# First-layer head outputs leave PSUM in one ScalarE copy: the square is taken from SBUF, and the sub-norm weight joins the product with the root

## The chip, the cores and the metric

The kernel runs on one core of one Trainium2 chip. The metric is device time in microseconds: 826.21 us is the median of three runs of the kernel before (824.39 to 827.17). A core has a matmul engine (TensorE; PE in the profile, PEld its weight loads), a vector engine (VectorE, DVE), an activation engine (ScalarE, ACT), a general engine (GpSimd, POOL) and a queue engine that issues DMAs (SyncE, SP). Each engine runs its own list of instructions in order and waits on semaphores for the others. Matmuls write to PSUM, which is cut into banks; everything else lives in SBUF.

## The reference

Two layers work on 512 latent tokens and 256 context tokens, 1024 wide. The change lies in the first layer, a differential attention with 8 heads, each with a 128-wide value and two 64-wide query/key pairs. Its core:

```python
o1 = sweep_attention(qq[..., 0, :], kk[..., 0, :], vv)
o2 = sweep_attention(qq[..., 1, :], kk[..., 1, :], vv)
o = o1 - lam * o2
o = rms_norm(o, subln_g) * (1.0 - lam_init)      # x * rsqrt(mean(x*x) + eps) * g, over a head's 128
o = o.reshape(o.shape[0], o.shape[1], BRANCH_WIDTH)
return (o * jax.nn.silu(gate)) @ w_out
```

Latent queries read all 768 keys, context queries only the 256 context keys. Around it stand the norms, adaptive shifts, scales and gates (`adaln`), and rotary positions. The second layer is a grouped-query attention with another code path, which the change does not touch.

## The kernel before, in words

**Precision.** Every matmul operand is split into a high and a low part (`h`, `whi`/`wlo`, `ah`/`al`, `vhi`/`vlo`), and three products are summed (`mm3`, L143 to L145; for the attention's second product `pv_mm`, L150). A split costs a cast on ScalarE and a subtraction on VectorE or GpSimd: weights at L213 (high) and L207 (low), values at L816 and after.

**PSUM.** There are four banks `bk` of 512 columns, handed out by least recent use: `trp()` takes one for a short time, `pj(n)` holds one as an accumulator until `close(o)` gives it back. Two double tiles `sc` hold attention scores. Whoever takes a bank waits until the last reader of its old contents is done.

**The first layer's attention.** For each head and each block of 128 queries, `unit` (L862 and after) makes both score sets (L880), takes their maximum (L885, VectorE), the exponential with its sum (L888, ScalarE), the reciprocal (L891), scales the first set (helper line L221, GpSimd), and combines `p = p0 + (-lambda/l1) p1` (L896, VectorE). The context queries have their own lines (L909 to L927). `tstep` transposes `p` (L945) and splits it: `ah` on ScalarE (L950), `al` on VectorE (L951). `mstep` multiplies with the values into a bank of 128 value rows by 256 queries. Each head has three such chunks of queries (two latent, one context): 24 outputs of 128x256 in all. After a head's last chunk, `subln` normalizes the 128x768 result: the column sum of squares by a matmul with ones (`colsum`, L378 to L382: cast on ScalarE, rest on GpSimd, two matmuls, result on all rows), logarithm (L979) and exponential (L981) on ScalarE give the root, VectorE multiplies (L982), and GpSimd multiplies with the gate `sz` (`gate_mul`, L839). The gate itself is made by `z_proj` (copy L850, and the steps L176 to L181 of a SiLU over ScalarE, VectorE and GpSimd). The last head has a form of its own, `subln_last` (L986 to L1000), in a piece of 512 and one of 256 columns, with the split for the out projection at once (L999, L1000); the other heads are split at L1026 and L1027.

**Order.** A planner in Python (`flow`) merges streams of steps (scores, transposes, second products, norms, and the adaptive rows at L736) by due times, and fills what is left with pieces of projections of later heads (queries and keys, values, gates). Then a scheduler at build time sets the order of each engine's list from priorities and its own estimate of durations. A changed instruction can therefore move others, on all engines.

**What the change touches.** `o` is the bank of a finished chunk, `gT[h]` the head's 128x768 result in SBUF, `ogs[h]` (`sq`) the tile of its squares, `subg` a column of 128 weights (the sub-norm's weight times 1 - lambda_init). At the end of a chunk ScalarE squares the bank (L968), VectorE multiplies it by `subg` (L969, through the helper `scaled`; `EG0 = 'v'` selects VectorE, and the profile shows it as L221 with `gT<-bk,subg`), and the bank is closed (L970).

Of the kernel before, what the change touches and what calls it, by code (L numbers as in the profile page):

```python
# [11 lines left out]
AF = mybir.ActivationFunctionType  # L12
ALU = mybir.AluOpType
# [54 lines left out]
EG0 = 'v'  # L68
# [8 lines left out]
def f32(ap):  # L77
    return ap.bitcast(F32)
# [3 lines left out]
def tile_backbone(  # L82
# [20 lines left out]
    nc = tc.nc  # L103
    uid = [0]

    def nm(s):
        uid[0] += 1
        return f"{s}_{uid[0]}"
# [15 lines left out]
    def trp():  # L124
        i = lru.pop(0)
        lru.append(i)
        return banks[i]

    def pj(n):
        i = lru.pop(0)  # L130
        o = banks[i][:, :n]
        held[id(o)] = (o, i)
        return o

    def close(o):
        lru.append(held.pop(id(o))[1])
# [10 lines left out]
    def pv_mm(o, vh, vl, c, ah, al, kt, first, last):  # L147
        terms = [(v, a, e) for v, a in ((vh, ah), (vl, ah), (vh, al)) for e in range(2)]
        for i, (v, a, e) in enumerate(terms):
            nc.tensor.matmul(o, v[:, kt + e, c], a[:, e * 256:e * 256 + 256], start=first and i == 0, stop=last and i == 5)  # L150
# [21 lines left out]
    subg = con.tile([P, 1], F32, name="subg")  # L172
# [44 lines left out]
    def scaled(eng, dst, src, s_):  # L217
        if eng == "a":
            nc.scalar.activation(dst, src, AF.Copy, scale=s_)
        else:  # L220
            (nc.vector if eng == "v" else nc.gpsimd).tensor_scalar(dst, src, s_, 1.0, ALU.mult, ALU.mult)  # L221
# [141 lines left out]
    def chunk(layer, tstep, mstep, kts, after, ts, ms):  # L363
        for i, kt in enumerate(kts):
            t = Step(lambda kt=kt: tstep(kt), 0.44, [(s_, LA[layer]) for s_ in after])
            if i:
                t.lag.append((ts[-1], LT[layer]))
            if len(ms) >= AB:
                t.lag.append((ms[-AB], 0.0))
            m = Step(lambda kt=kt: mstep(kt), 0.65, [(t, LM[layer])])  # L370
            ts.append(t)
            ms.append(m)
# [4 lines left out]
    def colsum(o, src, parts):  # L377
        hi, lo = parts  # L378
        nc.scalar.copy(hi, src)
        nc.gpsimd.tensor_tensor(lo, src, f32(hi), ALU.subtract)  # L380
        nc.tensor.matmul(o, ones_r, hi, start=True, stop=False)
        nc.tensor.matmul(o, ones_r, lo, start=False, stop=True)  # L382
# [53 lines left out]
    def htile():  # L436
        return hp.tile([P, T], F32R, tag="h", name=nm("h"), bufs=16)
# [277 lines left out]
    gT = [None] * KT  # L715

    with tc.tile_pool(name="t0", bufs=1) as t0:
# [118 lines left out]
        def gate_mul(h):  # L836
            done.add(h)
            if h in szt and (h, "o") in done:
                nc.gpsimd.tensor_tensor(gT[h], gT[h], szt[h], ALU.mult)  # L839
# [96 lines left out]
        def pv_steps(h, at, ch, after, ts, ms):  # L936
            kts = range(6) if ch < 2 else range(4, 6)
            st = {}

            def tstep(kt):  # L940
                tr = trp()
                for e in range(2):
                    j = kt + e - kts[0]
                    for i, a in enumerate(at):
                        nc.tensor.transpose(tr[:, e * 256 + i * P:e * 256 + (i + 1) * P], a[:, j * P:(j + 1) * P], ident)  # L945
                if h == 0 and ch == 0 and kt == 0:
                    t0.tile([P, 8], F32, name="pad_a")
                ah = t0.tile([P, 512], F32R, tag="ah", name=nm("ah"), bufs=AB)
                al = t0.tile([P, 512], F32R, tag="al", name=nm("al"), bufs=AB)
                nc.scalar.copy(ah, tr)  # L950
                nc.vector.tensor_tensor(al, tr, f32(ah), ALU.subtract)  # L951
                st[kt] = ah, al

            def mstep(kt):
                if kt == kts[0]:
                    st["o"] = pj(256)
                o = st["o"]
                ah, al = st[kt]
                vh, vl = vt[h]
                vc = slice((h % 2) * P, (h % 2) * P + P)  # L960
                pv_mm(o, vh, vl, vc, ah, al, kt, kt == kts[0], kt == kts[-2])
                if kt == kts[-2]:
                    if ch == 2:
                        pvdone.add(h)
                    sl = slice(ch * 256, ch * 256 + 256)
                    if ch == 0:
                        ogs[h] = t0.tile([P, T], F32, tag="sq", name=nm("sq"), bufs=1)
                    nc.scalar.activation(ogs[h][:, sl], o, AF.Square)  # L968
                    scaled(EG0, gT[h][:, sl], o, subg)  # L969
                    close(o)  # L970

            chunk(0, tstep, mstep, kts[::2], [after], ts, ms)

        def subln(h):
            sq, og = ogs[h], gT[h]
            for (a, b) in halves:
                o2 = pj(384)
                colsum(o2, sq[:, a:b], [t0.tile([P, 512], F32R, tag="tmp", name=nm("sqs"), bufs=3)[:, :b - a] for _ in range(2)])
                nc.scalar.activation(sq[:, a:b], o2, AF.Ln, scale=1.0 / P, bias=eps)  # L979
                close(o2)  # L980
            nc.scalar.activation(sq, sq, AF.Exp, scale=-0.5)  # L981
            nc.vector.tensor_tensor(og, og, sq, ALU.mult)  # L982
            done.add((h, "o"))
            gate_mul(h)

        def subln_last(a, b):  # L986
            h = KT - 1
            sq, og = ogs[h][:, a:b], gT[h][:, a:b]
            if a == 0:
                ghi.append(htile())  # L990
                glo.append(htile())
            o2 = pj(b - a)
            colsum(o2, sq, [t0.tile([P, 512], F32R, tag="tmp", name=nm("sqs"), bufs=3)[:, :b - a] for _ in range(2)])
            nc.scalar.activation(sq, o2, AF.Ln, scale=1.0 / P, bias=eps)
            close(o2)
            nc.scalar.activation(sq, sq, AF.Exp, scale=-0.5)
            nc.vector.tensor_tensor(og, og, sq, ALU.mult)
            VP[EGL].tensor_tensor(og, og, szt[h][:, a:b], ALU.mult)
            nc.scalar.copy(ghi[h][:, a:b], og)  # L999
            nc.vector.tensor_tensor(glo[h][:, a:b], og, f32(ghi[h][:, a:b]), ALU.subtract)  # L1000
# [30 lines left out]
        ogs = {}  # L1031
# [174 lines left out]
    for qi, (c, n) in enumerate(OUTC[:2]):  # L1206
# [4 lines left out]
        for m in order:  # L1211
            v = 0 if m < NQ else 1
            o = pj(n) if qi else o_pre[m]
# [60 lines left out]
    for i, m in enumerate(order):  # L1274
        o = pj(n)
# [11 lines left out]
    with tc.tile_pool(name="t1", bufs=1, side="right") as t1p:  # L1287
# [64 lines left out]
        for what, m in KV:  # L1352
# [7 lines left out]
            else:  # L1360
                if what == "v" and wv is None:
                    wv = (ws.get(10), ws.get(11))
                o = pj(256)
# [213 lines left out]
        for qi, (c, n) in enumerate(OUTC1):  # L1577
# [4 lines left out]
            for m in range(NQ):  # L1582
                o = pj(n) if qi else o_pre[m]
# [12 lines left out]
                if qi == 2:  # L1596
                    r = rstd_sum(ss[m][:, 2:3], ss[m][:, 0:1])
                    for j in (1, 0):
                        for h in range(2 if m == NQ - 1 else 1):
                            w_ = 256 if m == NQ - 1 else 512  # L1600
                            a = h * w_
                            sl = slice(j * 512 + a, j * 512 + a + w_)
# [90 lines left out]
```

## Time and profile before

| | us |
|---|---|
| runs (three) | 827.17, 824.39, 826.21 |
| median | 826.21 |
| span of the profiled execution | 822.0 |
| first layer's attention, from the first head output to the end of the last split | about 112 to 486 |
| L968, 24 squares on ScalarE, each | 0.384 |
| L221 on `gT`, 24 products on VectorE, each | 0.477 |
| L982, 7 products of 768 columns on VectorE, each | 0.95 to 2.04 |

The runs are timed without the profiler. For the profiled execution only its span is given, from its first to its last instruction; a time of its own beside it is not. Views of the profile are of that one execution. In a timeline row stand the start, the duration, engine, line, operation, output and inputs, shape, how many such instructions in a row, and in brackets the idle time of the engine before it with what ended it.

### The profile page before, as it was taken

To read this page: it belongs to the slowest core of one execution; us is meant where nothing else is said; L and a number is where in the kernel's file an instruction comes from. 1 tells how busy PE (TensorE), PEld (TensorE's weight loads), DVE (VectorE), ACT (ScalarE), POOL (GpSimd) and SP (SyncE) were. 2 spreads that over 40 slices of the span, in tenths; PEclk is the share of its full clock that TensorE was granted. 3 is DMA by queue.
4 is the path that set the end of the run, shared out by engine and by line. 5 is a ranking of instruction groups with operands and counts; after the bars stand their busy time and mean duration, and the time that the engine had idled before them with its cause. 6 is when DMAs were issued, how large, how long until landed. Compare 5 with 4: busy or idle time off the path is not lost. (4 is left out here: it accounts for less than half of the span.)

```text
span 822.0 us, 14412 instructions
## 1 busy us (share of the span) xinstructions
PE 792.7 (96%) x5482; PEld 703.0 (86%) x5482; DVE 482.3 (59%) x896; ACT 457.1 (56%) x1001; POOL 440.4 (54%) x538
## 2 busy tenths in 40 slices
PE   7999999999999999999999999999999999999997
PEld 5678897788887898787988898889999899898986
DVE  3425566754768524675458952579546566755534
ACT  6534357664575544765556852674446576666631
POOL 4544766856367744665822311587788656733101
PEclk9999999999999999999999999999999999999999
DMA  9934211122053321323330045033421210301102
GB/s 300 347 131 142 77 39 52 52 77 90 28 154 98 122 101 65 116 78 118 113 104 26 27 151 182 1 110 103 154 79 52 78 52 1 103 26 52 50 28 103
DMA packets 41540, 77.77 MB, mean 95 GB/s; under 512 B 3584, under 2 KB 18688, under 8 KB 41472
## 3 DMA queue, kind: packets, MB, share of 16 engines
q1 hardware_dynamic: 38048, 71.71, 26.4%
q10 hardware_dynamic: 3424, 5.15, 1.8%
q8 instruction: 43, 0.70, 0.3%
q14 instruction: 25, 0.20, 0.1%
HBM read 70.56 MB, written 2.10 MB: 88 GB/s over the span
## 5 line engine op out<-in xcount | busy, mean ns | idle before, releaser
L207 POOL TENSOR_TENSOR wlo<-raw,whi 128x256 fp32r<-128x256 f32 x200 | 152.0, 792 | 72.8 <-ACT whi L213 63.1
L143 PE MATMUL bk<-whi,h 128*128 128x256 f32 (+1 forms) x592 | 176.9, 302 | 1.1 <-ACT p L1459 0.8
L144 PE MATMUL bk<-wlo,h 128*128 128x256 f32 (+1 forms) x592 | 176.2, 299 | 0.2 <-DVE wlo L207 0.2
L145 PE MATMUL bk<-whi,h 128*128 128x256 f32 (+1 forms) x592 | 175.4, 299 | 0.2 <-DVE h L1272 0.2
L143 PE MATMUL bk<-h,whi 128*128 128x512 f32 (+2 forms) x416 | 147.4, 354 | 2.7 <-ACT sq L979 1.5
L144 PE MATMUL bk<-h,whi 128*128 128x512 f32 (+2 forms) x416 | 144.8, 348 | 0.0
L145 PE MATMUL bk<-h,wlo 128*128 128x512 f32 (+2 forms) x416 | 144.8, 348 | 0.0
L143 PEld LDWEIGHTS bk<-whi,h 128*128 128x128 f32 x592 | 112.6, 191 | 8.2 <-issue 2.8
L145 PEld LDWEIGHTS bk<-whi,h 128*128 128x128 f32 x592 | 112.0, 190 | 4.7 <-issue 0.8
L144 PEld LDWEIGHTS bk<-wlo,h 128*128 128x128 f32 x592 | 112.3, 190 | 3.9 <-DVE wlo L207 0.4
L221 POOL TENSOR_SCALAR p<-p,sm 128x768 f32<-128x768 f32 (+1 forms) x80 | 67.1, 842 | 76.5 <-DVE sm L1460 28.7
L143 PEld LDWEIGHTS bk<-h,whi 128*128 128x128 f32 x416 | 78.2, 188 | 15.1 <-issue 4.0
L213 ACT CAST whi<-raw 128x1024 fp32r<-128x1024 f32 x64 | 67.1, 1048 | 36.1 <-PE bk L144 17.7
L145 PEld LDWEIGHTS bk<-h,wlo 128*128 128x128 f32 x416 | 78.3, 188 | 8.8 <-issue 1.6
L144 PEld LDWEIGHTS bk<-h,whi 128*128 128x128 f32 x416 | 78.4, 188 | 7.2 <-issue 0.8
L888 ACT ACTIVATE p<-sc,sm 128x768 f32<-128x768 f32 (+1 forms) x68 | 59.7, 881 | 37.9 <-DVE sm L885 37.9
L885 DVE TENSOR_REDUCE sm<-sc 128x1 f32<-128x768 f32 (+1 forms) x68 | 60.3, 917 | 17.4 <-PE sc L880 17.3
L181 POOL TENSOR_TENSOR sz<-sz,za 128x384 f32<-128x384 f32 (+1 forms) x24 | 28.1, 1172 | 42.8 <-ACT za L180 42.7
L896 DVE SCALAR_TENSOR_TENSOR p<-p,sm,p 128x768 f32<-128x768 f32 (+1 forms) x34 | 40.1, 1179 | 16.5 <-POOL p L221 14.9
L1480 DVE TENSOR_TENSOR al<-bk,ah 128x512 fp32r<-128x512 f32 x48 | 32.6, 687 | 26.1 <-ACT ah L1479 25.9
L950 ACT CAST ah<-bk 128x512 fp32r<-128x512 f32 x56 | 31.7, 590 | 27.9 <-PE bk L945 24.4
L880 PE MATMUL sc<-qk,qk 64*128 64x384 f32 (+1 forms) x396 | 45.8, 354 | 1.1 <-ACT p L888 1.0
(247 smaller groups left out, 1693.0 us busy)
## 6 DMA issues: line engine op xcount, KB each, us to landing
raw<-in_a_w SPq DMA_DIRECT2D x30, 512.0 KB, 3.6
araw<-in_ada_w SPq DMA_DIRECT2D x12, 1024.0 KB, 5.6
raw<-in_b_w SPq DMA_DIRECT2D x20, 512.0 KB, 3.5
ag<-in_ada_w SPq DMA_DIRECT2D x32, 256.0 KB, 6.9
raw<-in_w_out SPq DMA_DIRECT2D x16, 512.0 KB, 3.5
sw<-qr ACTq DMA_DIRECT2D x32, 128.0 KB, 2.5
gw<-in_ada_w SPq DMA_DIRECT2D x8, 512.0 KB, 3.8
xt<-in_x SPq DMA_DIRECT2D x4, 512.0 KB, 5.3
```

What stands on the lines that cost most here:

```text
L143: nc.tensor.matmul(o, ahi, bhi, start=start, stop=False)
L144: nc.tensor.matmul(o, ahi, blo, start=False, stop=False)
L145: nc.tensor.matmul(o, alo, bhi, start=False, stop=stop)
L207: eng.tensor_tensor(dst[:, i:i + n], a[:, i:i + n], b[:, i:i + n], op)
L213: nc.scalar.copy(hi, r)
L221: (nc.vector if eng == "v" else nc.gpsimd).tensor_scalar(dst, src, s_, 1.0, ALU.mult, ALU.mult)
L880: prev = nc.tensor.matmul(sc[m][:, j if nk == T else m, :w], a[r, tok], b[r, c], start=i == 0, stop=i == 2)
L885: nc.vector.tensor_reduce(mx, scv, AX.XY if nk == T else AX.X, ALU.max, negate=True)
L888: nc.scalar.activation(pv_, scv, AF.Exp, bias=mx, accum_out=l[:, m:m + 1])
L896: nc.vector.scalar_tensor_tensor(ps_[0], pt, r, ps_[0], ALU.mult, ALU.add)
L950: nc.scalar.copy(ah, tr)
L1480: nc.vector.tensor_tensor(al, tr, f32(ah), ALU.subtract)
```

## The change

A head output leaves its bank through one copy on ScalarE, unweighted, and the bank is closed after it. The square is then taken on ScalarE from the copy in SBUF. The weight `subg` is applied later, in the product with the root, which becomes an instruction with three operands, (og x subg) x sq. The squares were of the unweighted output before, and are so still; the result is the same up to rounding.

```diff
@@ mstep, after the last product of a chunk
-                    nc.scalar.activation(ogs[h][:, sl], o, AF.Square)
-                    scaled(EG0, gT[h][:, sl], o, subg)
+                    nc.scalar.copy(gT[h][:, sl], o)
                     close(o)
+                    nc.scalar.activation(ogs[h][:, sl], gT[h][:, sl], AF.Square)
@@ subln (heads 0 to 6)
             nc.scalar.activation(sq, sq, AF.Exp, scale=-0.5)
-            nc.vector.tensor_tensor(og, og, sq, ALU.mult)
+            nc.vector.scalar_tensor_tensor(og, og, subg, sq, ALU.mult, ALU.mult)
             done.add((h, "o"))
@@ subln_last (head 7, two pieces)
-            nc.vector.tensor_tensor(og, og, sq, ALU.mult)
+            nc.vector.scalar_tensor_tensor(og, og, subg, sq, ALU.mult, ALU.mult)
             VP[EGL].tensor_tensor(og, og, szt[h][:, a:b], ALU.mult)
```

The lists of the engines differ from the first head output (about 112 us) to the end of the first layer (about 490 us); the second layer's order is the same in both. Names ending in a number are tiles by their running number. On ScalarE, at the first head's first output (`bk_70` is the finished bank, `p` the exponentials of the next block), the place itself reads:

```order
 L888 ACTIVATE p_1113,sm_1098<-sc_72,sm_1111 128x768
-L968 ACTIVATE sq_1218<-bk_70 128x256
+L968 COPY gT_896<-bk_70 128x256
 L888 ACTIVATE p_1119,sm_1098<-sc_73,sm_1117 128x768
+L970 ACTIVATE sq_1218<-gT_896 128x256
 L850 COPY sz_1324<-bk_71 128x384
```

The copy stands where the square stood, and the square an exponential later. On VectorE, from about 136 to 144 us, around the first head's product with the root (L982; `za` is a step of the gate path, `p_1515` a block that is combined, the L885 are reductions of scores):

```order
+L885 TENSOR_REDUCE sm_1513<-sc_72 128x1
 L179 TENSOR_SCALAR za_1409<-sz_1324,za_1409 128x384
-L885 TENSOR_REDUCE sm_1513<-sc_72 128x1
 L885 TENSOR_REDUCE sm_1519<-sc_73 128x1
-L982 TENSOR_TENSOR gT_896<-gT_896,sq_1218 128x768
-L891 RECIPROCAL sm_1500<-sm_1500 128x1 x2
+L982 TENSOR_SCALAR gT_896<-gT_896,subg,sq_1218 128x768
+L891 RECIPROCAL sm_1500<-sm_1500 128x1
+L179 TENSOR_SCALAR za_1467<-sz_1324,za_1467 128x384
+L891 RECIPROCAL sm_1500<-sm_1500 128x1
 L895 TENSOR_TENSOR sm_1500<-sm_1500,nlam 128x1
 L896 TENSOR_SCALAR p_1515<-p_1521,sm_1500,p_1515 128x768
```

The second gate step (`za_1467`) moved from behind the combine L896 to ahead of it. On TensorE at about 450 us, the column sum of the seventh head's squares (`sqs_4833`) and what follows it, before:

```order
L945 MATMUL bk_70<-ident,p_4777 128x128
L382 MATMUL bk_68<-sqs_4833,ones_r 128x384
L143 MATMUL bk_68<-h_288,whi_4531 128x384
L144 MATMUL bk_68<-h_289,whi_4531 128x384
L145 MATMUL bk_68<-h_288,wlo_4532 128x384
```

and after:

```order
L945 MATMUL bk_71<-ident,p_4777 128x128
L382 MATMUL bk_68<-sqs_4833,ones_r 128x384
L880 MATMUL sc_72<-qk_4602,qk_4600 128x256 x2
L880 MATMUL sc_72<-qk_4603,qk_4600 128x256 x2
L880 MATMUL sc_72<-qk_4602,qk_4601 128x256 x2
L150 MATMUL bk_70<-ah_4882,vhi_4363 128x256 x2
```

The last gate projection (`whi_4531`), which followed the column sum and takes its bank, now stands behind score matmuls of the last head's context and a run of second products. On ScalarE at the end of the layer (`h_5216` is the last head's high part, `whi_5368` a weight of the out projection), the difference is:

```order
 L994 ACTIVATE sq_5004<-bk_70,eps 128x512
+L968 COPY gT_4684<-bk_71 128x256
 L996 ACTIVATE sq_5004<-sq_5004 128x512
-L999 COPY h_5216<-gT_4684 128x512
-L968 ACTIVATE sq_5004<-bk_71 128x256
+L970 ACTIVATE sq_5004<-gT_4684 128x256
 L379 COPY sqs_5248<-sq_5004 128x256
 L213 COPY whi_5368<-raw_5366 128x1024
+L999 COPY h_5216<-gT_4684 128x512
```

The cast L999 of the last head's large piece moved behind the square of its small piece and the weight cast L213.

## The prediction

> **What bounds the kernel now.** I read the page first, then the chain that ended last, then the busy time of the stretch that the change touches (the first layer's attention, 107 to 492 us), then what TensorE waited for in it.
>
> ```profile
> span 822.0 us, 14412 instructions
> PE 792.7 (96%) x5482; PEld 703.0 (86%) x5482; DVE 482.3 (59%) x896; ACT 457.1 (56%) x1001; POOL 440.4 (54%) x538
> PE 30%; ACT 1%; DVE 1%; issue 0%; POOLq 0%; DVEq 0%; POOL 0%; ACTq 0%
> ```
>
> TensorE is busy for 96% of the span and holds nearly all that the chain can name. The other engines have some 40% of their time free. They matter where TensorE has to wait for one of them. By stretch (columns: length, then busy us of PE, PEld, DVE, ACT, POOL, granted clock, DMA share, GB/s):
>
> ```profile
> 107.00:492.00 385.00, 374.96 (x2677) 327.89 (x2676) 243.84 (x419) 229.03 (x491) 212.06 (x210) 1.00 0.25 85
> 200.00:250.00 50.00, 50.00 (x325) 41.19 (x324) 34.41 (x59) 31.80 (x71) 30.61 (x34) 1.00 0.27 80
> 450.00:480.00 30.00, 26.89 (x205) 25.28 (x205) 25.07 (x41) 22.19 (x46) 7.64 (x7) 1.00 0.05 18
> ```
>
> In the stretch of the change TensorE stands still for 385.00 - 374.96 = 10.0 us. That is all this change can win: 1.2% of the span. From 200 to 250 us it never stops, though VectorE and ScalarE are busier there than on average, since projections fill every gap. In the tail, 450 to 480 us, it loses 3.1 us, a third of the whole. What ended those waits, 110 to 500 us (us in total, times, longest):
>
> ```profile
> PE bk L945 <- DVE al L951: 2.0, 2, 1.6
> PE bk L143 <- ACT sq L979: 1.5, 1, 1.5
> PE sc L880 <- ACT p L888: 1.0, 1, 1.0
> PE bk L736 <- DVE al L951: 1.0, 1, 1.0
> PE bk L150 <- DVE al L951: 0.9, 2, 0.5
> PE sc L143 <- ACT p L888: 0.7, 1, 0.7
> PE bk L143 <- DVE gT L221: 0.7, 1, 0.7
> PE bk L945 <- DVE p L896: 0.6, 1, 0.6
> PE bk L736 <- DVE gT L221: 0.6, 1, 0.6
> PE sc L145 <- DVE h L1027: 0.4, 1, 0.4
> ```
>
> Only two of the waits, 0.7 + 0.6 us, end with the weight product from PSUM that the change removes (`gT`, L221). The others end with the low parts `al`, exponentials `p`, L896 and the norm's logarithm L979.
>
> **The change part by part.** Prices (ns minimum/median/maximum, first and last start):
>
> ```profile
> L968 ACT ACTIVATE sq<-bk x24: 371/384/425, 112.3 to 478.9; 128x256 f32<-128x256 f32 x24
> L221 DVE TENSOR_SCALAR gT<-bk,subg x24: 469/477/486, 112.7 to 479.5; 128x256 f32<-128x256 f32 x24
> L816 ACT CAST vhi<-bk x21: 353/373/636, 69.6 to 418.4; 128x256 fp32r<-128x256 f32 x18, 128x512 fp32r<-128x512 f32 x3
> L999 ACT CAST h<-gT x2: 406/514/622, 478.3 to 485.3; 128x512 fp32r<-128x512 f32 x1, 128x256 fp32r<-128x256 f32 x1
> L896 DVE SCALAR_TENSOR_TENSOR p<-p,sm,p x34: 469/1019/2045, 89.4 to 471.3; 128x768 f32<-128x768 f32 x32, 128x256 f32<-128x256 f32 x2
> L1027 DVE TENSOR_TENSOR h<-gT,h x7: 936/950/951, 457.5 to 466.7; 128x768 fp32r<-128x768 f32 x7
> ```
>
> *The bank comes free sooner.* Before, a head output's bank is held through a ScalarE square (0.384 us) and then a VectorE product (0.477) in VectorE's queue. After, one ScalarE copy frees it. No row has that copy; the nearest, the eviction cast of 256 columns (L816), takes 0.373, so the copy ends when the square ended. What it is worth shows at the two places:
>
> ```profile
> 154.54 0.38 ACT L968 ACTIVATE sq<-bk 128x256 f32<-128x256 f32 x1
> ...
> 156.70 0.47 DVE L221 TENSOR_SCALAR gT<-bk,subg 128x256 f32<-128x256 f32 x1
> ...
> 157.23 0.39 PE L143 MATMUL bk<-h,whi 128*128 128x256 f32 x1 [0.71 <-DVE gT L221]
> ```
> ```profile
> 370.76 0.38 ACT L968 ACTIVATE sq<-bk 128x256 f32<-128x256 f32 x1 [2.44 <-PE bk L150]
> ...
> 371.95 1.07 PE L736 MATMUL bk<-araw,s 128*32 128x512 f32 x8 [0.59 <-DVE gT L221]
> ```
>
> At the first place the copy would end at 154.9, long before TensorE wants the bank (157.23 - 0.71 = 156.5); at the second at 371.1, before 371.95 - 0.59 = 371.4. Both waits go: -0.7 - 0.6 = **-1.3 us**. None of the other ten rows stands close enough behind either to take its place, but for the transposes at 155.64, which come below.
>
> *VectorE loses 24 products*, 24 x 0.477 = 11.4 us. The nine sub-norm products become products with three operands. The nearest rows are L896 (1.019) against L1027 (0.950): +0.07 each, +0.6 in all. VectorE's share of the stretch falls from 243.8/385 = 63% to 233.0/385 = 61%. The row `al` (2.0 + 1.0 + 0.9 us) could gain 0.48 for each of its five waits that has such a product ahead of it in the queue, 2.4 in all, and 0 otherwise. In the order of the changed kernel the longest of them (1.6 us) still stands behind the same two reductions, and the one of L736 where it stood. I take **0**, with -2.4 as the far end.
>
> *ScalarE gains 24 Squares from SBUF.* The nearest row from SBUF with 256 columns is L999's short one, 0.406; from PSUM L968's, 0.384. So 24 x 0.38 = 9.1 to 24 x 0.41 = 9.8 us, less 24 x (0.384 - 0.373) = 0.3 on the copy: some +9.2, and ScalarE goes from 229.0/385 = 59% to 62%. The Square stands behind the copy, so nothing on TensorE needs it until the column sum of the head. But what is queued behind it on ScalarE does: the next exponential (the wait of L880 and `sc` L143, 1.0 + 0.7) and the next cast `ah`, ahead of `al`. The bounds are 0 (every Square in a free moment; ScalarE has 38% free) and 9.2 (all on the path). The rows of 200 to 250 us, where ScalarE is at 64% and no wait reaches TensorE, are nearest to the first. I take **+0.5**: about one Square and a third on the path.
>
> [...]
>
> *The order moves.* Build-time ordering puts other instructions ahead, on all engines, between 112 and 490 us. Two moves touch rows of waits. First, at 144 us a VectorE step of the gate path (L179) now stands ahead of a combine instead of behind it:
>
> ```profile
> 144.10 0.55 DVE L179 SCALAR_TENSOR_TENSOR za<-sz,za 128x384 f32<-128x384 f32 x1
> 145.29 1.00 POOL L181 TENSOR_TENSOR sz<-sz,za 128x384 f32<-128x384 f32 x1 [2.26 <-ACT za L180]
> ...
> 153.54 2.04 DVE L896 SCALAR_TENSOR_TENSOR p<-p,sm,p 128x768 f32<-128x768 f32 x1 [2.15 <-POOL p L221]
> 155.64 0.88 PE L945 MATMUL bk<-ident,p 128*128 128x128 f32 x6 [0.61 <-DVE p L896]
> ```
>
> L179 comes 1.0 us sooner, so POOL's L181, which waited 2.26 for its chain, and POOL's later product `p`, for which VectorE waited 2.15, come sooner too: L896 ends earlier by up to 1 us, and TensorE's 0.61 goes: **-0.6**. The combine that it passes is later by 0.55; I put that under the moved rows below. If POOL is held by its own products instead, the gain is 0.
>
> Second, the tail:
>
> ```profile
> 449.68 0.42 PE L382 MATMUL bk<-sqs,ones_r 128*128 128x384 f32 x1
> 451.40 0.92 ACT L888 ACTIVATE p<-sc,sm 128x768 f32<-128x768 f32 x1
> 451.57 0.45 PE L143 MATMUL bk<-h,whi 128*128 128x384 f32 x1 [1.47 <-ACT sq L979]
> 465.07 0.38 PE L145 MATMUL sc<-whi,h 128*128 128x256 f32 x1 [0.43 <-DVE h L1027]
> 469.16 0.51 PE L150 MATMUL bk<-al,vhi 128*128 128x256 f32 x2 [0.49 <-DVE al L951]
> 470.59 0.39 PE L143 MATMUL sc<-whi,h 128*128 128x256 f32 x1 [0.72 <-ACT p L888]
> ```
>
> These four lose 1.47 + 0.43 + 0.49 + 0.72 = 3.1 us. In the new order the projection no longer follows the column sum: context scores do, which wait for an exponential (0.92) instead of the logarithm behind two casts. With that exponential moved ahead it ends near 451.1, against 450.1 for the column sum's end: 1.0 left of 1.47. The casts and reductions of the last head come earlier on ScalarE and VectorE; walking the new order with the durations above I find 0.1 left of the split, 0 of `al`, and 0.2 of the last exponential. Together 1.3 of 3.1: **-1.8**. Bounds: -3.1 (all goes), or +1.5 (the first wait comes a second time, behind the scores).
>
> Other moved rows may bring waits of their own. The stretch has 12 waits of about 0.8 us in 385 us; I take one more, **+0.8**, between 0 and four of them (+3.2).
>
> *Sum:* -1.3 + 0 + 0.5 - 0.6 - 1.8 + 0.8 = -2.4 us; span 822.0 - 2.4 = 819.6. No time of the profiled execution beside its span is given; the median of the runs, 826.21, lies 4.2 above the span, and I carry that over: **823.8 us**. The second layer's order is the same in both and gets 0. What a measurement of this kernel can tell from no change is about 0.3%, 2.5 us, so 823.7 and 828.7 are the marks.
>
> **The rivals.**
>
> *No change.* The freed banks and the reorder buy nothing: TensorE waits next for `al` or an exponential at the same places, since both engines keep their queue. For it: only 1.3 us of the 10.0 ends with the removed product, and the gains of 2.4 from the order rest on walking it by hand. Against it: both banks' copies are done 0.2 to 1.6 us before they are asked for. With -1.3 + 0.8 it gives 821.5 + 4.2 = 825.7.
>
> *Slower: ScalarE comes last.* One mechanism: a Square stands ahead of an exponential or a cast that TensorE waits for. Against the gains of 3.7 and the 0.8 of moved rows, the sign turns at (3.7 - 0.8)/0.38 = 8 Squares; with 16 of the 24 it is -2.9 + 6.1 = +3.2, 829.4 us. For it: three of the ten rows of waits end with ScalarE already, and in the tail ScalarE is at 22.19/30 = 74%, with no projections left to fill. The last head is the place:
>
> ```profile
> 478.27 0.62 ACT L999 CAST h<-gT 128x512 fp32r<-128x512 f32 x1 [1.55 <-DVE gT L998]
> 480.32 1.05 ACT L213 CAST whi<-raw 128x1024 fp32r<-128x1024 f32 x1 [0.27 <-PE bk L145]
> ...
> 482.12 0.28 PE L143 MATMUL sc<-whi,h 128*128 128x256 f32 x1
> ```
>
> L999 now comes behind a copy, a Square, a cast and the weight cast L213, which itself waits for TensorE: it ends at 480.32 + 1.05 + 0.62 = 482.0 instead of 478.9. TensorE first uses it at 482.12, or 2.0 us later with the 14 matmuls that now stand ahead (374.96/2677 = 0.14 each): about 2 us of slack, and less for the low part that VectorE makes from it. Against it: from 200 to 250 us no wait at all.
>
> *Faster by more.* `al` gains its 2.4 and no new wait comes: -2.4 - 2.4 - 0.8 = -5.6, 820.6 us.
>
> **How the numbers follow.** The forecast (gains and a few new waits, 822.5 to 825) has 0.38, no change (to 828.7) 0.23, slower 0.25, faster by more 0.14. The forecast lies on the mark and gives 0.24 of its share to faster. So faster by over 0.3%: 0.38; within: 0.37; slower: 0.25. The range leaves out the far half of the slow case and little below: 820.5 to 830.5. The likeliest case's own is 822.5 to 825.
>
> **What would show it.** In the profile after: no `gT` L221 rows on VectorE, 24 copies near 0.37 and 24 Squares near 0.40 us; no wait for a head output's bank at L143 or L736; ScalarE's busy time in the stretch near 238 us, VectorE's near 233; fewer than 1.5 us of waits from 448 to 472. Wrong if the waits of TensorE that end with ScalarE grow beyond 4 us, or if the stretch's idle time stays at 10 us.

## The result and the profile after

Over 20 runs of each, measured side by side, the changed kernel takes 823.96 us at the median (821.66 to 825.94) and the kernel before 825.22 (823.88 to 827.81). The ratio is 0.9982, with a 95% interval of 0.9974 to 0.9989: faster by 0.18%, or 1.5 us, which is less than the 0.3% that the prediction set as its mark. The forecast of 823.8 us lies 0.2 from it. As will be seen, that closeness is luck: two errors of more than 2 us each cancel in it.

The page of the profile after:

```profile
span 822.5 us, 14396 instructions
PE 793.0 (96%) x5482; PEld 702.5 (85%) x5482; DVE 471.4 (57%) x872; ACT 465.0 (57%) x1025; POOL 439.4 (53%) x538
```

VectorE is busy 10.9 us less (482.3 before), ScalarE 7.9 us more (457.1). The new instructions (ns minimum/median/maximum):

```profile
L968 ACT COPY gT<-bk x24: 355/373/408, 113.3 to 478.7; 128x256 f32<-128x256 f32 x24
L970 ACT ACTIVATE sq<-gT x24: 405/418/473, 114.4 to 479.5; 128x256 f32<-128x256 f32 x24
L982 DVE SCALAR_TENSOR_TENSOR gT<-gT,subg,sq x7: 1014/1324/1494, 140.8 to 456.7; 128x768 f32<-128x768 f32 x7
```

The Square from SBUF takes 418 ns against 384 from PSUM, 34 ns more.

The two spans, 822.0 before and 822.5 after, go the other way than the medians, so the span is not the place to look. A better frame runs from the first attention score (L880, 81.20 before, 82.10 after) to the first transpose of the next layer (L1261). It holds the same 3006 matmuls in both. Busy time by stretch, before and then after (columns: length, then busy us of PE, PEld, DVE, ACT, POOL, granted clock, DMA share, GB/s):

```profile
81.20:521.30 440.10, 430.06 (x3006) 375.02 (x3006) 266.46 (x454) 250.19 (x538) 238.65 (x254) 1.00 0.26 88
81.20:160.00 78.80, 75.51 (x508) 64.71 (x508) 49.89 (x84) 45.60 (x99) 55.65 (x55) 1.00 0.17 59
160.00:345.00 185.00, 185.00 (x1305) 159.09 (x1304) 108.64 (x190) 106.27 (x221) 108.90 (x112) 1.00 0.28 92
345.00:425.00 80.00, 78.44 (x557) 67.70 (x556) 46.27 (x77) 43.36 (x91) 51.45 (x48) 1.00 0.33 107
425.00:521.30 96.30, 91.12 (x642) 83.51 (x642) 61.66 (x107) 54.96 (x130) 22.65 (x41) 1.00 0.25 87
```
```profile
82.10:522.10 440.00, 430.32 (x3006) 375.02 (x3006) 255.00 (x430) 257.97 (x562) 238.66 (x254) 1.00 0.27 88
82.10:160.00 77.90, 75.30 (x509) 64.95 (x508) 49.33 (x79) 46.89 (x103) 55.29 (x55) 1.00 0.19 58
160.00:345.00 185.00, 184.28 (x1294) 157.08 (x1293) 104.92 (x178) 108.65 (x229) 106.78 (x111) 1.00 0.28 93
345.00:425.00 80.00, 77.03 (x547) 66.76 (x546) 42.46 (x72) 43.41 (x89) 51.45 (x47) 1.00 0.31 100
425.00:522.10 97.10, 93.72 (x662) 86.23 (x661) 58.29 (x103) 59.02 (x142) 25.14 (x42) 1.00 0.27 93
```

Length less TensorE's busy time is its idle time: 10.04 us before, 9.68 after. By stretch it went from 3.3 to 2.6, from 0 to 0.7, from 1.6 to 3.0, and in the tail from 5.2 to 3.4 us. So the last stretch gained 1.8 us and the start 0.7, and the two middle stretches lost 2.1. In this frame the change is worth 0.1 us of length and 0.4 us of idle time. What TensorE waited for after, 107 to 500 us (us in total, times, longest):

```profile
PE sc L880 <- ACT p L888: 2.0, 2, 1.0
PE bk L736 <- DVE al L951: 1.4, 1, 1.4
PE bk L736 <- ACT whi L213: 1.1, 1, 1.1
PE bk L150 <- DVE al L951: 0.9, 2, 0.5
PE bk L945 <- DVE p L896: 0.9, 1, 0.9
PE bk L144 <- DVE wlo L207: 0.8, 1, 0.8
PE bk L945 <- DVE al L951: 0.6, 2, 0.4
PE sc L145 <- DVE h L1027: 0.6, 1, 0.6
PE bk L945 <- ACT gT L968: 0.5, 1, 0.5
PE bk L143 <- ACT arow L739: 0.4, 1, 0.4
PE bk L382 <- POOL sqs L380: 0.3, 1, 0.3
```

Gone are the waits that ended with the product from PSUM (0.7 + 0.6), with the logarithm L979 (1.5) and with the last exponential (`sc` L143, 0.7). The largest that are new or have grown, beside the 0.96 us of an exponential at 453.51, stand at L736, the adaptive rows. The places, from the timeline of TensorE and of the DMA queue:

```profile
146.33 0.33 PE L945 MATMUL bk<-ident,p 128*128 128x128 f32 x1 [0.89 <-DVE p L896]
350.47 1.06 PE L736 MATMUL bk<-araw,s 128*32 128x512 f32 x8 [1.39 <-DVE al L951]
375.51 8.77 SPq L726 DMA_DIRECT2D araw<-in_ada_w  x2
382.79 1.07 PE L736 MATMUL bk<-araw,s 128*32 128x512 f32 x8 [1.06 <-ACT whi L213]
433.28 0.66 PE L945 MATMUL bk<-ident,p 128*128 128x128 f32 x4 [0.52 <-ACT gT L968]
453.51 0.63 PE L880 MATMUL sc<-qk,qk 64*128 64x256 f32 x6 [0.96 <-ACT p L888]
467.08 0.38 PE L145 MATMUL sc<-whi,h 128*128 128x256 f32 x1 [0.57 <-DVE h L1027]
```

At 382.79 the name of the releaser misleads. The weights of these rows (`araw`, 1 MB) have one buffer, so their DMA is issued when the group before has read it (374.39 + 1.07 = 375.46), at 375.51 (the row's two DMAs start there and at about 384). The 12 DMAs of `araw` land 4.9 to 7.1 us after issue in this execution. Before, the next group came 12.7 us after the issue (373.08 to 385.80); now it comes 7.3 us after. A second profile of the same kernel names the DMA at the same place (`araw`, 1.2 us). At 350.47 the low part `al` is late because a row in front of it in VectorE's list waits 4.96 us for another DMA:

```profile
346.30 0.69 DVE L773 TENSOR_TENSOR sw<-sw,rope 128x512 f32<-128x512 f32 x1 [4.96 <-DMA sw<-qr]
346.90 0.95 DVE L885 TENSOR_REDUCE sm<-sc 128x1 f32<-128x768 f32 x1
347.77 1.18 DVE L982 SCALAR_TENSOR_TENSOR gT<-gT,subg,sq 128x768 f32<-128x768 f32 x1
348.87 0.94 DVE L885 TENSOR_REDUCE sm<-sc 128x1 f32<-128x768 f32 x1
349.74 1.87 DVE L951 TENSOR_TENSOR al<-bk,ah 128x512 fp32r<-128x512 f32 x3
```

Before, TensorE's wait at this group was 1.0 us (348.33). VectorE waited for that DMA then too (1.52 us, until 344.65), but the second reduction L885 between the product L982 and the low part is new. Neither place waits for a head output. Both differ by the moved order.

One place does show the bank itself. At 431 us the kernel before stood still for 1.57 us (its two rows, and then a row of after that follows the 433.28 above):

```profile
431.38 0.66 PE L945 MATMUL bk<-ident,p 128*128 128x128 f32 x4 [1.57 <-DVE al L951]
431.38 0.47 DVE L221 TENSOR_SCALAR gT<-bk,subg 128x256 f32<-128x256 f32 x1
```
```profile
434.30 0.66 PE L945 MATMUL bk<-ident,p 128*128 128x128 f32 x4 [0.37 <-DVE al L951]
```

Before, the square of this head output was done at 430.31, but its product stood in VectorE's queue until 431.38, so the transposes L945 waited for the bank of a low part instead. After, that low part comes no sooner: it ends 1.5 us after the matmuls in front (L749) in both kernels. But the copy frees the head output's bank 0.5 us after them. The transposes now wait 0.52 us for the copy and 0.37 for the low part, 0.7 us less in all.

### The profile page after: what moved, and what is told of

Its sections match the earlier page's. It is cut to its first block, busy times and chain, and to the rows that moved or that the text cites. A ratio compares the mean times of both kernels' runs of the same rounds, so it can differ in the third digit from the quotient of the medians.

```text
span 822.5 us, 14396 instructions
## 1 busy us (share of the span) xinstructions
PE 793.0 (96%) x5482; PEld 702.5 (85%) x5482; DVE 471.4 (57%) x872; ACT 465.0 (57%) x1025; POOL 439.4 (53%) x538
## 5 line engine op out<-in xcount | busy, mean ns | idle before, releaser
L143 PE MATMUL bk<-whi,h 128*128 128x256 f32 (+1 forms) x592 | 176.4, 301 | 1.2 <-ACT p L1459 0.8
L143 PE MATMUL bk<-h,whi 128*128 128x512 f32 (+2 forms) x416 | 147.0, 354 | 0.9 <-DVE al L1480 0.5
L143 PEld LDWEIGHTS bk<-whi,h 128*128 128x128 f32 x592 | 111.8, 189 | 8.6 <-issue 2.5
L143 PEld LDWEIGHTS bk<-h,whi 128*128 128x128 f32 x416 | 78.2, 188 | 13.6 <-issue 4.4
L888 ACT ACTIVATE p<-sc,sm 128x768 f32<-128x768 f32 (+1 forms) x68 | 59.9, 882 | 45.8 <-DVE sm L885 45.8
L213 ACT CAST whi<-raw 128x1024 fp32r<-128x1024 f32 x64 | 67.1, 1049 | 32.9 <-PE bk L144 14.4
L885 DVE TENSOR_REDUCE sm<-sc 128x1 f32<-128x768 f32 (+1 forms) x68 | 60.3, 918 | 17.3 <-PE sc L880 17.3
L896 DVE SCALAR_TENSOR_TENSOR p<-p,sm,p 128x768 f32<-128x768 f32 (+1 forms) x34 | 41.0, 1207 | 13.1 <-POOL p L221 10.9
L1480 DVE TENSOR_TENSOR al<-bk,ah 128x512 fp32r<-128x512 f32 x48 | 32.6, 688 | 26.1 <-ACT ah L1479 25.9
L880 PE MATMUL sc<-qk,qk 64*128 64x384 f32 (+1 forms) x396 | 45.1, 353 | 2.0 <-ACT p L888 2.0
L951 DVE TENSOR_TENSOR al<-bk,ah 128x512 fp32r<-128x512 f32 x56 | 37.5, 684 | 16.5 <-ACT ah L950 16.3
```

The lines of the kernel that those rows point to most:

```text
L143: nc.tensor.matmul(o, ahi, bhi, start=start, stop=False)
L213: nc.scalar.copy(hi, r)
L880: prev = nc.tensor.matmul(sc[m][:, j if nk == T else m, :w], a[r, tok], b[r, c], start=i == 0, stop=i == 2)
L885: nc.vector.tensor_reduce(mx, scv, AX.XY if nk == T else AX.X, ALU.max, negate=True)
L888: nc.scalar.activation(pv_, scv, AF.Exp, bias=mx, accum_out=l[:, m:m + 1])
L896: nc.vector.scalar_tensor_tensor(ps_[0], pt, r, ps_[0], ALU.mult, ALU.add)
```

## The experiments

Theory: the gain comes from the bank that VectorE no longer holds; it shows in the tail; the moved order adds or takes a few waits elsewhere. Rivals: VectorE's relief pays; ScalarE's Squares cost; the moved order is all there is.

### Both kernels again

The changed kernel once more:

> The changed kernel once more, to have it beside the other experiments and to get a second profile of it. All theories: ratio to the kernel before 0.998 (0.9974 to 0.9989 in the first measurement). The second profile shows how far two profiles of one kernel differ: the first pair had spans of 822.0 before and 822.5 after, against medians that fell by 1.3 us. Expected: TensorE's idle time from 107 to 492 us again near 9.7 us (385.00 - 375.32), the waits of the same lines within 0.3 us each, and differences of up to 1 us from the time before the first attention score.

Measured: 823.97 us, ratio 0.9984 (0.9972 to 0.9996). Idle time in the frame is 9.8 us, and the waits are the same within 0.1 us, but for one of 0.4 us that is gone. And the kernel before:

> The kernel before once more, for a second profile of it and for the size of a difference that is none. All theories: ratio 1.000, within 0.001. In the profile the stretch from the first attention score to the first transpose of the next layer (521.3 - 81.2 = 440.1 us in its first profile; 440.0 and 439.9 in the two of the changed kernel) shows how far one profile can be trusted: if it is again 440.1, the change gains 0.15 us there by the profile and the rest of the measured 1.3 us lies elsewhere; if it is up to 1 us longer, the first profile of before was a good one.

Measured: 825.07 us, ratio 1.0002 (0.9991 to 1.0012). Its profile, the frame and its last stretch:

```profile
81.10:522.90 441.80, 431.75 (x3007) 376.60 (x3007) 267.29 (x454) 250.41 (x538) 238.35 (x254) 1.00 0.27 88
425.00:522.90 97.90, 92.73 (x644) 85.01 (x643) 61.78 (x107) 55.03 (x130) 22.71 (x41) 0.98 0.24 86
```

The frame is 1.7 us longer than in the first profile of the same kernel, all of it in busy time (431.75 against 430.06), and the idle time is the same 10.05. The granted clock says why; the same 10 us in the first and in the second profile of the kernel before:

```profile
430.00:440.00 10.00, 8.62 (x62) 8.23 (x63) 9.00 (x20) 5.40 (x13) 2.50 (x3) 1.00 0.00 0
```
```profile
430.00:440.00 10.00, 8.59 (x53) 8.10 (x54) 7.69 (x19) 5.45 (x13) 2.54 (x3) 0.83 0.00 0
```

In the second profile the clock is 0.83 in this one slice of the frame, and 53 matmuls fit in it instead of 62. So two profiles of one kernel differ by more than the change is worth, and idle time, not length, is what can be compared. In the table below idle time is the length of a stretch less TensorE's busy time, us:

| kernel | ratio to before | start to 160 | 160 to 345 | 345 to 425 | 425 to next layer | all |
|---|---|---|---|---|---|---|
| before | 1 | 3.3 | 0.0 | 1.6 | 5.2 | 10.0 |
| before, again | 1.0002 | 3.3 | 0.0 | 1.6 | 5.2 | 10.1 |
| changed | 0.9982 | 2.6 | 0.7 | 3.0 | 3.4 | 9.7 |
| changed, again | 0.9984 | 2.8 | 0.3 | 3.3 | 3.4 | 9.8 |
| early copy alone | 0.9996 | 2.3 | 1.3 | 2.7 | 3.6 | 10.0 |
| weight alone | 0.9987 | 2.6 | 0.0 | 1.5 | 5.2 | 9.3 |
| Squares twice | 0.9945 | 2.6 | 0.4 | 0.0 | 3.5 | 6.5 |
| row moved | 0.9988 | 3.2 | 0.7 | 2.0 | 3.4 | 9.4 |
| two buffers | 0.9979 | 3.0 | 0.3 | 2.7 | 3.4 | 9.5 |
| ScalarE holds the bank | 0.9947 | 2.7 | 0.3 | 0.4 | 3.0 | 6.4 |
| before, priority | 1.0026 | 3.2 | 2.5 | 1.5 | 5.1 | 12.3 |
| changed, priority | 0.9927 | 1.8 | 0.0 | 0.1 | 3.0 | 4.9 |
| before, due time | 1.0092 | 3.3 | 0.1 | 5.1 | 5.2 | 13.7 |
| changed, due time | 1.0033 | 2.8 | 0.3 | 4.9 | 3.4 | 11.5 |

The last stretch takes two values: 5.1 to 5.2 us where VectorE reads the head output from its bank, 3.0 to 3.6 where it does not. The place at 431 us divides the same way: 1.55 to 1.57 us in the five kernels of the first kind, 0.52 to 0.54 and 0.37 in the others (0.81 in all where ScalarE holds the bank). The other stretches follow no such rule.

### One half of the change at a time

The early copy, with the weight still in a product of its own:

```diff
@@ the kernel before, mstep
-                    nc.scalar.activation(ogs[h][:, sl], o, AF.Square)
-                    scaled(EG0, gT[h][:, sl], o, subg)
+                    nc.scalar.copy(gT[h][:, sl], o)
                     close(o)
+                    nc.scalar.activation(ogs[h][:, sl], gT[h][:, sl], AF.Square)
+                    scaled(EG0, gT[h][:, sl], gT[h][:, sl], subg)
```

> Early copy alone: copy to SBUF, bank closed, Square from SBUF, and then the weight product as an instruction of its own on VectorE, in place, from SBUF; the product with the root is the two-operand one again. VectorE's 24 products are back, but none holds a bank. The order on the other engines is nearly that of the changed kernel (44 of some 4870 rows of TensorE differ, 6 of ScalarE). Theory of the bank and of the order: as the changed kernel, 0.998 of before, within 0.001 of it. Rival, VectorE's relief: the 24 x 0.4 = 10 us of VectorE work come back, so the gain is gone: 1.000.

Measured: 824.15 us, ratio 0.9996 (0.9986 to 1.0006), which shares 0.9986 to 0.9996 with the interval of the changed kernel beside it (0.9972 to 0.9996) and holds 1.000 as well. By the times the two expectations can't be told apart. The profile is clearer for the tail: VectorE has its 24 products again (354 ns each, from SBUF), and the tail still lost only 3.6 us. So the tail's gain does not need VectorE's relief.

The weight alone, with the bank held by the square and by a VectorE copy:

```diff
@@ the changed kernel, mstep
-                    nc.scalar.copy(gT[h][:, sl], o)
-                    close(o)
-                    nc.scalar.activation(ogs[h][:, sl], gT[h][:, sl], AF.Square)
+                    nc.scalar.activation(ogs[h][:, sl], o, AF.Square)
+                    nc.vector.tensor_copy(gT[h][:, sl], o)
+                    close(o)
```

> Weight moved alone: the square is taken from PSUM on ScalarE as before, VectorE copies the bank unweighted (so the bank is held by both as before), and the weight is applied in the product with the root. ScalarE's load is that of before; VectorE's is that of before and 9 x 0.07 more. The order is close to before's (181 rows of TensorE differ, against 652 for the changed kernel). Theory of the bank: the two waits that end with VectorE's reading of the bank (0.7 + 0.6 us) stay, 1.000. Rival, the order: what moved in the tail comes back with the order of before, so 1.000 too, unless the weight alone reorders it, then any of 0.998 to 1.002. Rival, weight product is dear: 1.001.

Measured: 824.85 us, ratio 0.9987 (0.9973 to 1.0001), which allows no change as well as the whole gain. Its waits from 440 to 500 us begin with the two of the kernel before:

```profile
PE bk L143 <- ACT sq L979: 1.5, 1, 1.5
PE sc L143 <- ACT p L888: 0.7, 1, 0.7
```

The tail is that of before (5.2 us). Together the two halves show that the early copy makes the tail's gain. They do not divide the gain in time, which is too small for these intervals.

### ScalarE's load

```diff
@@ the changed kernel, mstep: the Square is done twice
                     nc.scalar.activation(ogs[h][:, sl], gT[h][:, sl], AF.Square)
+                    nc.scalar.activation(ogs[h][:, sl], gT[h][:, sl], AF.Square)
```

> The changed kernel with each Square done twice on ScalarE (the second writes the same values): 24 x 0.418 = 10.0 us more on ScalarE behind the early copy, TensorE's order close to the changed kernel's (276 rows differ of 4870). Theory that Squares are covered: 10.0 us more cost what the first 24 were put at, about 0.5 us; ratio 0.9985 of before, ScalarE's waits at TensorE up by under 1 us. Rival, ScalarE comes last: a third of them or more reach TensorE, +3.3 us or more, ratio 1.002 or above, and then the first 24 Squares cost the change a similar sum too.

Measured: 820.68 us, ratio 0.9945 (0.9933 to 0.9956): with 24 more Squares of 0.418 us each on ScalarE (10.0 us in all; its busy time in the frame is 265.04 us against 257.97) the kernel is faster than both, which neither theory expected.

```profile
80.80:518.10 437.30, 430.77 (x3006) 376.20 (x3006) 257.46 (x430) 265.04 (x586) 237.66 (x254) 1.00 0.26 89
345.00:425.00 80.00, 80.00 (x575) 69.20 (x576) 43.13 (x78) 47.94 (x104) 47.31 (x46) 1.00 0.34 107
```

No wait of TensorE's matmuls ends with a Square, and those that end with an exponential (L888) are 2.0 us, as in the changed kernel. From 345 to 425 us, where ScalarE has 4.5 us more to do than in the changed kernel, TensorE does not stop at all: the waits of L736 are gone (1.4 and 1.1 us in the changed kernel), since the order put two low parts ahead of the product L982, and the group after the DMA a little later (7.7 us behind its issue instead of 7.3). So, as far as the waits show, ScalarE's load is covered even when it is doubled, and of the 3.0 us of this stretch 2.5 hang on the place of two groups of matmuls. The order moved with the added Squares, so the faster time says nothing for or against them.

The other way to load ScalarE leaves the bank to it alone:

```diff
@@ the changed kernel, mstep
                     nc.scalar.copy(gT[h][:, sl], o)
-                    close(o)
-                    nc.scalar.activation(ogs[h][:, sl], gT[h][:, sl], AF.Square)
+                    nc.scalar.activation(ogs[h][:, sl], o, AF.Square)
+                    close(o)
```

> The changed kernel, but the Square is taken from PSUM again, behind the copy: ScalarE alone holds the bank, 0.37 + 0.38 us instead of 0.37. VectorE is as in the changed kernel; 456 rows of TensorE differ from it. Theory of the bank: at the two places of before (157.2 and 372.0 us) the bank would come free 0.4 us later than in the changed kernel, which costs 0.2 us at the second at most: ratio to before 0.9985 to 0.9990. Rival, that what counts is where the rows of the adaptive weights and the low parts fall: any ratio from 0.995 to 1.001, and the waits of L736 in the profile say which.

Measured: 819.90 us, ratio 0.9947 (0.9935 to 0.9959). The bank is held longer than in the changed kernel by the Square (0.396 us at the median) and the kernel is 0.4% faster than it. In the frame:

```profile
81.30:518.40 437.10, 430.69 (x3006) 376.28 (x3006) 254.17 (x430) 255.22 (x562) 240.21 (x254) 1.00 0.26 89
425.00:518.40 93.40, 90.39 (x638) 82.81 (x638) 56.43 (x100) 55.70 (x134) 24.35 (x40) 1.00 0.25 88
```

No L736 waits here either; one wait, 0.8 us at 430, ends with the Square, which now reads the bank; the second wait of that place, for the low part, is gone, so that the longer hold costs nothing there (0.81 against 0.52 + 0.37). The strict form of the theory, that every tenth of a microsecond at the bank counts, falls; what the tail depends on in all these runs is that VectorE's queue is not between the head output and its bank.

### The adaptive rows

One due time moved (`{12: -0.4}.get(i, 0)` added to the place of step i), so that the two groups stand further apart:

> The changed kernel with one due time of an adaptive row moved earlier by 0.4 of a third of a head, so that two groups of its matmuls (L736) stand some 80 rows apart on TensorE instead of 53, near 375 and 383 us; 111 rows of TensorE differ. In the changed kernel the second of them waits 1.06 to 1.22 us, because its DMA is issued 7.3 us before, behind the first group, which reads the only buffer; before it was issued 12.7 us ahead and nothing waited. Theory that the change gave its gain back at this DMA: the wait goes, -1.1 us against the changed kernel, ratio to before 0.9970. Rival, that TensorE then waits for something else at the same place (the bank behind the low parts, the weight cast): 0.9984 as before.

Measured: 823.66 us, ratio 0.9988 (0.9979 to 0.9996), not the expected 0.9970. The group of 382.79 now comes 13.7 us after its DMA and waits for nothing, which bears out what it waited for:

```profile
372.66 0.38 SPq L726 DMA_DIRECT2D araw<-in_ada_w  x1
386.35 1.05 PE L736 MATMUL bk<-araw,s 128*32 128x512 f32 x4
```

Idle time in 345 to 425 us fell by 0.9 us, but the time did not follow: a new wait of 0.5 us for L896 came. A second buffer instead (`bufs=2` for `araw`):

> The changed kernel with two buffers for the adaptive rows' weights, so that their DMA is issued one group sooner; the matmuls keep their distance of 53 rows; 404 rows of TensorE differ. Theory of the DMA: no wait on it, -1.1 us against the changed kernel, ratio to before 0.9970; the 1.4 us at 350 us that end with the low part stay. Rival: as in the experiment beside it, 0.9984.

Measured: 823.24 us, ratio 0.9979 (0.9970 to 0.9987), which holds both expectations. The DMA is not waited for any more, but the low parts are, for longer than before:

```profile
PE bk L736 <- DVE al L951: 1.8, 1, 1.8
PE bk L150 <- DVE al L951: 1.6, 2, 1.1
PE bk L143 <- DVE al L951: 1.5, 1, 1.5
```

Both experiments remove the wait they aim at and lose it to others, as each also moves the order.

### The same change in two other orders

A pair with one priority changed in both kernels, the third number of `HOT0` from 0 to 100:

> The kernel before with one number of the order changed and nothing else: the priority of the second products is 100 instead of 0. 556 rows of TensorE move, about as many as the change under study moves (652); no instruction is added or removed. Theory that the order decides: the time moves by up to 0.5% either way although the work is the same. Rival, that the order is worth little and the change's own instructions decide: within 0.1% of before.

> The changed kernel with the same number changed (100 instead of 0): the pair with the run beside it is the change once more, in another order. If the change's own worth is what the first pair showed, the ratio of this one to that one is 0.998 to 0.9985. If the order decides, the ratio of the pair lies anywhere from 0.994 to 1.006 and says nothing on the change alone; the idle time of TensorE between the first attention score and the next layer then accounts for most of the difference.

Measured: 827.48 us, 1.0026 (1.0014 to 1.0038), without the change and 819.46 us, 0.9927 (0.9909 to 0.9945), with it. The ratio of the pair is 0.9927/1.0026 = 0.990, outside both expectations.

```profile
82.60:527.80 445.20, 432.86 (x3006) 377.23 (x3006) 267.79 (x454) 249.32 (x538) 237.80 (x254) 0.99 0.25 87
```
```profile
81.30:516.10 434.80, 429.94 (x3006) 374.77 (x3006) 255.12 (x430) 258.00 (x562) 240.08 (x254) 1.00 0.26 89
```

Idle time is 12.3 against 4.9 us. And a pair with one due time changed in both (`{10: 0.25}.get(i, 0)`):

> The kernel before with one due time of an adaptive row later by 0.25 of a third of a head; the order of TensorE differs in 2676 rows, mostly in which weights and tiles follow. Theory that the order decides: any ratio from 0.995 to 1.005. Rival: within 0.1% of before.

> The changed kernel with the same due time later: the third pair. Change's own worth: 0.998 to 0.9985 of the run beside it. Order decides: any ratio of the pair from 0.994 to 1.006.

Measured: 833.36 us, 1.0092 (1.0075 to 1.0109), and 828.08 us, 1.0033 (1.0019 to 1.0046); 0.994 for the pair. The first of these is beyond every expectation. In its profile the frame is 7.6 us longer than before: 3.7 us of idle time and 4.0 us of busy time (434.1 against 430.1). The idle time is one wait, here in the kernel without the change, 340 to 430 us:

```profile
PE bk L143 <- DVE arow L742: 3.7, 1, 3.7
```

The busy time goes with the granted clock, which is lowered from 350 to 360 us (0.83) and from 430 to 450 (0.89 and 0.94) in this profile and not in the first one of before. Whether the wait or the order brings that on is open.

A number of the planner that has nothing to do with head outputs moves the time from -0.55% (0.9927 against 0.9982) to +0.92%. Yet in each of the three orders the changed kernel is the faster of its pair, and in each its last stretch has 1.8 to 2.2 us less idle time, some 0.2 to 0.3% of the time. What goes beyond that differs from order to order. The changed kernel with the other priority, 819.46 us, is faster than both kernels of the case.

## Why the prediction was right, and where not

**The two bank waits** (-1.3) went, at both places. A third place was put at nothing: the longest wait for `al` (1.6 us) was to stay, since it "still stands behind the same two reductions". The low part did stay as late, but the early copy gave the transposes another bank: 1.57 became 0.52 + 0.37, another -0.7.

**VectorE's 24 products** (0, with -2.4 as the far end): busy time fell by 11.5 us in the frame (forecast 10.8), and the waits for `al` fell from 3.9 to 2.9 us. With the products back (early copy alone) they are 3.0, so that 1.0 is not due to the relief. Zero was right, as far as the profile shows.

**The Squares** (+0.5): the Square costs 0.418 against the 0.406 of the nearest row, the copy 0.373, as taken. In the changed kernel no matmul's wait ends with a Square, and twice as many cost nothing that shows. The term was too large, and the slower rival, which needed eight of them on the path, has nothing in the runs for it. ScalarE's busy time from 107 to 492 us, 236.7, was forecast as 238. The cast L999 was a close call as described: it ended at 481.81 + 0.62 = 482.4, and no wait followed.

**The tail** (-1.8): 1.3 of 3.1 us were to be left of the four waits; 0.96 + 0.57 = 1.5 are, so -1.6. The exponential that the context scores wait for was put at 1.0 and took 0.96; the split was put at 0.1 and took 0.57, more than the 0.43 of before; the last exponential was put at 0.2 and is gone. This is the step that held best. That the last stretch of the frame gained just the forecast 1.8 is chance: it is made of these -1.6, of the -0.7 at 431 us, which was not forecast, and of 0.6 more for a weight's low part at 488.88. What the walk by hand did not say is why; the halves say that it is the early copy. At 431 us it is the shorter hold itself. None of the four waits of the tail ended with a head output's bank, so there, as far as the waits show, the copy worked through the order that it brings about.

**L896 at 155.64** (-0.6): gone, but the combine that was to be 0.55 late cost 0.89 at 146.33. The prediction put it under the moved rows.

**Moved rows** (+0.8): this is the term that was mis-sized. Idle time changed by -0.36 us. With -1.3 and -0.7 for the banks, -0.6 for L896 and -1.6 in the tail, that leaves +3.8 for everything else, where the forecast had 0.8 + 0.5. The list: 1.06 at the adaptive rows' DMA, 0.4 more at 350, 0.5 at 363, 0.9 at 146, 0.6 more for a weight's low part, 0.4 for a row of L739 and smaller ones. Even the upper bound, +3.2, was a little low. The step from "one wait of median size" was an average over an order that nobody had looked at (and the "12 waits of about 0.8 us" are 12 rows with 14 waits, of 0.7). All these places could have been walked in the new order like the tail, above all the 7.3 us between a DMA and its use.

**The signs.** Most came as said: copies of 0.373 us, VectorE at 232.8 us of the stretch, no wait for a head output's bank at L143 or L736 (but the one at L945). The waits from 448 to 472 are 1.53 us, where fewer than 1.5 were to be left. But one sign of being wrong was that the stretch's idle time stays at 10 us, and from 107 to 492 us it went from 10.0 only to 9.7. The parts were mostly seen; their sum, -2.4, was not there.

**The sum.** A change of -2.4 us was forecast and 1.3 (of medians) to 1.5 (by the ratio) measured. That the time was hit to 0.2 us is luck. The forecast was a span of 819.6 us with 4.2 carried over to the time. The span of the changed kernel is 822.1 us at the median of its 20 runs (822.5 in the profile), 2.5 more than forecast, and its time is only 1.9 us longer than its span, 2.3 less than carried over. The 4.2 set a rather short execution against the median of three runs, which lies 1.0 us above the median of the 20; run by run, the time of the kernel before is 2.3 to 2.4 us longer than the span (29 runs), that of the changed kernel 1.8 to 1.9 in every run. So 0.4 to 0.5 us of the measured gain lie outside the span, where no profile shows anything. It is not the bank, since the kernel before with the other due time holds the bank as before and has 1.8 to 1.9 too. What sets it is open.

The rest of the gain lies in the span, 0.6 us between the medians of the runs measured together (822.1 against 822.7), and the 0.4 of idle time is of that size. The profiles can't show it any finer. From the frame's end to the last instruction, where the order is the same, the kernel before took 822.0 - 521.3 = 300.7 us and 824.5 - 522.9 = 301.6, the changed one 300.4 in both of its profiles. Why identical work should gain 0.3 to 1.2 us there is open; the two profiles of the kernel before, with and without the slice at 0.83, differ in busy time by 1.7 us (431.75 against 430.06), which is more than all that is to be explained.

**The chances.** "Faster by more", for `al` and no new waits, had 0.14. Two kernels with the same early copy and other orders, 0.9927 and 0.9947, came out that way, by losing the waits at L736 and not by `al`. In idle time "no change" (0.23), worth -0.5, was nearest to the measured -0.4: the freed waits were replaced, though at other places than the same ones.

## What to carry to other kernels

Where a scheduler orders the work at build time, judge a small change by two or three orders of the same pair: here numbers of the planner alone moved the kernel before by up to 0.9% and the changed one by up to 0.55% either way, and the change was worth 0.2, 1.0 and 0.6%. Look for the part that shows in every order (here the tail, where VectorE's queue stood between a result and its bank) and keep it; then tune the rest again. And when rows are moved, check the distance from each single-buffered DMA to its first use in the new order, not only the engines' waits.

## What was not expected

From 430 to 440 us the granted clock is 0.83 in one profile of the kernel before and 1.00 in the other, and TensorE's busy time in the frame is 431.75 against 430.06 us. The two profiles of one kernel differ by 2.5 us in span (822.0 and 824.5) at equal idle time (10.04 and 10.05) and nearly equal medians (825.22 and 825.07).

Work added to an engine at 59% made the kernel faster by 0.4% (820.68 against 823.97, measured together). Of the 3.2 us of idle time that went, 3.0 lie in the stretch where the order moved two groups of matmuls.
